# A second value copy in strips, keys interleaved on partitions, and dumps issued from SyncE in the long sequence's branch B

## The chip, the cores and the metric

The kernel runs on one core of one Trainium2 chip. The metric is the time of one execution on the device, in microseconds, as the median of several runs. The core has a matrix engine (TensorE, PE in the profile), a vector engine (VectorE, DVE), an activation engine (ScalarE, ACT), a general engine (GpSimd, POOL) and a queue engine (SyncE, SP). DMAs are issued from the queues of SP, ACT or POOL; an engine's instructions, DMA issues among them, run in the order in which they stand in its program.

## The reference

One encoder layer is computed for two sequences, a long one of 1024 tokens and a short one of 512, each with 1024 features:

```python
z = xn @ w_in                      # q_A k_A v_A q_B k_B v_B gate_A gate_B
o_a = _gqa_attention(qa, ka, va)   # 8 heads of 64, full attention
o_b = _neighbourhood_attention(qb, kb, vb, rpb)
mix = (sigmoid(ga) * (o_a @ w_proj_a) + sigmoid(gb) * (o_b @ w_proj_b)) @ w_out
h = x + mix
y = rmsnorm(h + square(relu(rmsnorm(h) @ w_up)) @ w_down)
```

Branch B is the part in question. The tokens lie on a grid 64 wide, so the long sequence has 16 rows. Each token attends, in 8 heads, to a window of 8 rows by 16 columns around it, clamped at the edges; a learned bias is added to the scores, a softmax follows, and its weights multiply the values:

```python
s = einsum('bqhd,bkhd->bhqk', qi, kb) * scale + bias
s = where(mask, s, NEG_INF)
p = softmax(s, axis=-1)
o = einsum('bhqk,bkhd->bqhd', p, vb)
```

## The kernel before

**Stages.** The two sequences are run one after the other by `run`, the short one first (`NB` = 1), the long one second (`NB` = 2); the MLP of both follows. For each sequence there are projections and sweeps of branch A for two groups of heads (`g` = 0, 1), then branch B, then the gated merge. The change touches branch B of the long sequence and, before it, its two branch A sweeps. Nearly all matrix products are made in pieces that are rounded to a high and a low part, so every operand is split first: ACT copies the high part, DVE subtracts it to get the low one.

**Values.** `values` (L637) computes the values of branch B for a tile of 128 tokens and stores them, high and low half of 64 floats each, in the DRAM tensor `vd` of tokens x 8 heads x 128. These stores go out on ACT's queue.

**Branch A's sweep** (L759 and on) works through 8 units for each group in the long sequence, 4 heads by 2 query blocks. In its gaps a `Fill` object feeds matmuls of the gates (`gate`, L439), whose weights SP loads into the three buffers of `rawp`; ACT and DVE split them.

**Branch B's units.** A unit is a head and a strip `j` of 16 query columns; its keys lie in a strip of 32 columns. The long sequence has 8 x 4 = 32 units; queries come in two halves of 128 (`hf`), each with 12 rows of 32 keys (`nkey` = 384). The loop at L1174 runs, for step `i`:

- `s_unit(i)` (L1008): POOL adds bias and mask (`bms`); TensorE makes the scores (`sbs`, four matmuls); DVE adds the bias and takes the maximum (`sbss`, `nmbs`); ACT takes Exp (`pbs`, L1065); DVE takes a reciprocal and POOL multiplies by it (L1068).
- The weights must then be turned so that keys lie on partitions. The last 8 units are turned by TensorE in `t_unit` (`ptbs`). The first 24, the set `moved`, take a **detour**: `turn` (L1072) has DVE transpose blocks of 32 x 32 (L1077) and then dumps the whole tile to DRAM (`tbs`, 384 KB, a DMA on POOL's queue, L1079); `fetch_t` (L1081) reads it back with the blocks in place (`bhs`), in four DMAs of 32 partitions on SP's queue (L1088).
- `prep_v` (L936) loads the unit's strip of values (`vss`) from `vd`, in four DMAs on SP, one for each band `a` of 32 partitions (L942). Partition `a * 32 + c` holds the key in row `4k + a`, column `c`.
- `t_unit` (L1094) splits the fetched weights, high part on ACT (L1099), low part on DVE (L1100), and `v_unit` (L1120) multiplies them with the values (`obs`).

`turn(i-1)` is called inside `s_unit(i)`, between the maxima and the Exps; `fetch_t(i-2)` comes right behind `s_unit(i)`; `t_unit` of a moved unit comes three steps after its `s_unit`, and `v_unit` one step later. Between them stand pieces of gate products (`fill.pull`) and, in two steps of every eight, the projections of the next pair of heads (`qkproj`). The buffers that matter: `pbs` has two, `bhs` three.

**What sets the order.** In branch B TensorE's order is that of the source, by hand (`mul`, L211). The orders of the other engines are made at compile time, from what each step is thought to take, and may differ from the source. `note` and `behind` (L186, L191) hold some of them: the instructions noted for an engine must come ahead of those issued inside `behind` for it. The loads of raw weights are noted for SP; the fetches and strips are issued behind them.

Of the kernel before, what the change touches and what calls it, by code (L numbers as in the profile page):

```python
# [11 lines left out]
F32 = mybir.dt.float32  # L12
# [6 lines left out]
P = 128  # L19
# [3 lines left out]
GRID_W = 64  # L23
# [38 lines left out]
def encoder(ctx: ExitStack, tc: tile.TileContext, xs, outs, w):  # L62
    nc = tc.nc
# [122 lines left out]
    def note(engine, op):  # L186
        if held_pe:
            firm[engine].append(op.ins)

    @contextmanager  # L190
    def behind(engine):  # L191
        with ExitStack() as st:
            for ins in firm[engine]:
                st.enter_context(tc.issue_after(ins))
            yield
        firm[engine].clear()
# [222 lines left out]
    def run(tr, nxt, first):  # L419
        N, x, T, NT, NB = tr.N, tr.x, tr.T, tr.NT, tr.NB  # L420
# [2 lines left out]
        halves = rows // 8  # L423

        vd = dram.tile([T, 8, P], F32, name=f"vd{N}")
        zg = [dram.tile([D, T], F32, name=f"zg{N}_{i}") for i in range(2)]
        oad = dram.tile([4 * P, T], F32, name=f"oad{N}")
        obd = dram.tile([4 * P, T], F32, name=f"obd{N}")
# [99 lines left out]
        for g in range(2):  # L528
# [230 lines left out]
            with phase(f"phA{N}_{g}") as ph:  # L759
                units = [(h, qb) for h in range(4) for qb in range(NB)]  # L760
                PP = {}

                def s_tile(u, j):
                    h, qb = u
                    nm = f"{N}_{g}_{h}_{qb}_{j}"
                    q0 = (qb * 4 + j) * P
                    lhs = qT[h % 2][:, h // 2, q0 : q0 + P]
                    s = big(f"s{nm}")[:, :T]
                    for kb in range(NB):
                        ks = slice(kb * 512, kb * 512 + 512)  # L770
                        nc.tensor.matmul(s[:, ks], lhs, kT[:, 0, ks], start=True, stop=False)
                        nc.tensor.matmul(s[:, ks], lhs, kT[:, 1, ks], start=False, stop=True)  # L772
                    nm_ = sml.tile([P, 1], F32, tag="nm", name=f"nm{nm}")
                    nc.vector.tensor_reduce(nm_, s, axis=AX.X, op=ALU.max, negate=True)  # L774
                    p = ph.tile([P, T], F32, tag="P", name=f"p{nm}", bufs=8)
                    l = sml.tile([P, 1], F32, tag="l", name=f"l{nm}")
                    nc.scalar.activation(p, s, AF.Exp, bias=nm_, accum_out=l)  # L777
                    rl = sml.tile([P, 1], F32, tag="rl", name=f"rl{nm}")
                    nc.vector.reciprocal(rl, l)  # L779
                    nc.gpsimd.tensor_scalar(p, p, rl, 1.0, op0=ALU.mult, op1=ALU.mult)  # L780
                    PP[u, j] = p

                o_of = {}

                def pv(u, kc, hi, lo):
                    h, qb = u
                    if kc == 0:
                        o_of[u] = mm(f"o{N}_{g}_{h}_{qb}")
                    o = o_of[u]
                    nc.tensor.matmul(o, vhl[:, kc, :], hi, start=(kc == 0), stop=False)  # L790
                    nc.tensor.matmul(o, vhl[:, kc, :], lo, start=False, stop=(kc == NT - 1))
                    if kc == NT - 1:
                        r0 = (g * 4 + h) * HD
                        finish_o(o, 512, oad[r0 : r0 + HD, qb * 512 : qb * 512 + 512], ph, f"A{N}_{g}_{h}_{qb}")

                for j in range(4):
                    s_tile(units[0], j)
                    fill.pull(2)
                queue = []
                LAG = 2  # L800
                for ui, u in enumerate(units):
                    h, qb = u
                    if first:
                        bias_row(g * 4 + ui)
                        if g == 0 and ui == 1:
                            early["a"] = load_a(1)
                        if g == 0 and ui == 2:
                            early["v"] = load_v(1, slot)
                    nxt_u = units[ui + 1] if ui + 1 < len(units) else None
                    sdone = 0  # L810
                    for kc in range(NT):
                        pt = mm(f"pT{N}_{g}_{h}_{qb}_{kc}")
                        for j in range(4):
                            nc.tensor.transpose(  # L814
                                pt[:, j * P : (j + 1) * P], PP[u, j][:, kc * P : (kc + 1) * P], ident
                            )
                        hi = ph.tile([P, 512], F32R, tag="pth", name=f"pth{N}_{g}_{h}_{qb}_{kc}", bufs=3)
                        lo = ph.tile([P, 512], F32R, tag="ptl", name=f"ptl{N}_{g}_{h}_{qb}_{kc}", bufs=3)
                        nc.scalar.activation(hi, pt, AF.Copy)  # L819
                        nc.vector.tensor_tensor(lo, pt, hi.bitcast(F32), op=ALU.subtract)  # L820
                        queue.append((u, kc, hi, lo))
                        if nxt_u is not None:
                            while sdone < 4 and kc >= ((0, 1, 3, 4) if NB == 2 else (0, 0, 1, 2))[sdone]:
                                s_tile(nxt_u, sdone)
                                sdone += 1

                        fill.pull(1 if NB == 1 or kc % 4 < 3 else 0)
                        if len(queue) > LAG:
                            pv(*queue.pop(0))
                fill.drain()  # L830
                for item in queue:
                    pv(*item)
# [80 lines left out]
        with phase(f"phB{N}") as ph:  # L913
# [22 lines left out]
            def prep_v(h, j):  # L936
                if h not in strips:
                    strips[h] = slot([P, 4, rows // 4, P], F32R, f"vs{N}_{h}")
                v = strips[h]
                c0 = (0, 8, 24, 32)[j]  # L940
                for a in range(4):
                    nc.sync.dma_start(  # L942
                        v[a * 32 : a * 32 + 32, j, :, :].bitcast(F32),
                        vd[:, h, :].rearrange("(k a c) d -> a c k d", a=4, c=GRID_W)[a, c0 : c0 + 32],
                    )
# [62 lines left out]
            def s_unit(u, before=None):  # L1008
# [47 lines left out]
                for hf, (sb, nm_) in enumerate(sums):  # L1056
                    nm = f"{N}_{h}_{j}_{hf}"
                    l = sml.tile([P, 1], F32, tag="l", name=f"lb{nm}")
                    p = pm[:, :, hf] if u in moved else pm[:, hf * nkey : (hf + 1) * nkey]
                    to, of = p, sb  # L1060
                    if u in moved:
                        to = p.rearrange("p b k i -> p k b i")
                        of = sb.rearrange("p (k b i) -> p k b i", b=4, i=32)
                    with behind("ACT"):
                        nc.scalar.activation(to, of, AF.Exp, bias=nm_, scale=-1.0, accum_out=l)  # L1065
                    rl = sml.tile([P, 1], F32, tag="rl", name=f"rlb{nm}")
                    nc.vector.reciprocal(rl, l)
                    nc.gpsimd.tensor_scalar(p, p, rl, 1.0, op0=ALU.mult, op1=ALU.mult)  # L1068
                    ps.append(p)
                PT[u] = pm if u in moved else ps  # L1070

            def turn(u):  # L1072

                h, j = u
                pm = PT[u]
                blocks = pm.rearrange("p b f k i -> p (b f k) i")
                tc.keep_in_program_order(nc.vector.transpose(blocks, blocks))  # L1077
                PT[u] = dram.tile([P, 4, halves * nkc * 32], F32, name=f"tb{N}_{h}_{j}")
                nc.gpsimd.dma_start(PT[u], pm.rearrange("p b f k i -> p b (f k i)"))  # L1079

            def fetch_t(u):  # L1081

                h, j = u
                hl = ph.tile([P, 2, 4, halves, nkc, 32], F32R, tag="bh", name=f"bh{N}_{h}_{j}", bufs=3)
                turned = PT[u].rearrange("(a i) b w -> b i a w", i=32)
                with behind("SP"):
                    for b in range(4):
                        nc.sync.dma_start(  # L1088
                            hl[b * 32 : b * 32 + 32, 1].rearrange("p a f k i -> p a (f k i)").bitcast(F32),
                            turned[b],  # L1090
                        )
                PT[u] = hl

            def t_unit(u):  # L1094
# [79 lines left out]
            for i in range(n + 4 - NB):  # L1174
# [8 lines left out]
                    next(pa)  # L1183
                if i < n:
                    late = i > 0 and units[i - 1] in moved
                    s_unit(units[i], partial(turn, units[i - 1]) if late else None)
                    if i > 1 and units[i - 2] in moved:
                        fetch_t(units[i - 2])
                    h, j = units[i]
                    if j == 1 and h < 7:  # L1190
                        if moved:
# [768 lines left out]
```

## Time and profile before

| what | us |
|---|---|
| median of 3 runs | 2142.17 |
| lowest, highest | 2140.59, 2144.18 |
| the profiled execution's own time | 2144.53 |
| its span, first to last instruction | 2142.7 |
| branch A of the long sequence, `g` = 0 and `g` = 1 (from the timeline) | 453 to 575, 640 to 771 |
| the 24 detour units of branch B (from the timeline) | 798 to 1000 |

The span is that of one execution taken by the hardware profiler. In its timelines a row is start, duration, engine, source line, operation, tiles written and read, count, and in brackets the idle time in front of it and what ended that. "PEld" is the loading of weights into TensorE, "SPq", "ACTq" and "POOLq" are the queues' own issues of DMAs, and "issue" stands where the profile shows nothing that was waited for. A tile's name is followed by `s`, `s1` or the like for the sequence; numbers are left out.

### The profile page before, as it was taken

To read this page: it belongs to the slowest core of one execution; us is meant where nothing else is said; L and a number is where in the kernel's file an instruction comes from. 1 tells how busy PE (TensorE), PEld (TensorE's weight loads), DVE (VectorE), ACT (ScalarE), POOL (GpSimd) and SP (SyncE) were. 2 spreads that over 40 slices of the span, in tenths; PEclk is the share of its full clock that TensorE was granted. 3 is DMA by queue.
4 is the path that set the end of the run, shared out by engine and by line. 5 is a ranking of instruction groups with operands and counts; after the bars stand their busy time and mean duration, and the time that the engine had idled before them with its cause. 6 is when DMAs were issued, how large, how long until landed. Compare 5 with 4: busy or idle time off the path is not lost.

```text
span 2142.7 us, 32014 instructions
## 1 busy us (share of the span) xinstructions
PE 2102.9 (98%) x10871; PEld 1841.3 (86%) x10871; DVE 1484.2 (69%) x2793; ACT 1141.0 (53%) x2487; POOL 374.0 (17%) x470
## 2 busy tenths in 40 slices
PE   9999999999999999989999999999999999999998
PEld 8888778988897888877888899999999988888886
DVE  6665786767657756766882877778777777659662
ACT  6664653767656645544531566566655633334442
POOL 2232310323233215533200200003000000000000
PEclk9999999999999999999999999999999999999999
DMA  6437557520122136666572666578544799688561
GB/s 190 133 97 212 156 159 252 184 73 25 54 80 70 42 95 190 206 206 184 176 247 101 209 193 192 164 252 208 159 145 158 260 353 341 213 274 279 165 206 59
DMA packets 337002, 372.95 MB, mean 174 GB/s; under 512 B 33471, under 2 KB 269639, under 8 KB 336839
## 3 DMA queue, kind: packets, MB, share of 16 engines
q1 hardware_dynamic: 296695, 296.17, 44.6%
q10 hardware_dynamic: 31072, 45.11, 6.0%
q0 software_dynamic: 9072, 29.63, 4.7%
q8 instruction: 86, 1.41, 0.3%
q14 instruction: 77, 0.63, 0.1%
HBM read 274.29 MB, written 97.32 MB: 173 GB/s over the span
## 4 chain that ended last, share of the span: by engine, by line
PE 52%; DVE 1%; issue 0%; DMA 0%; ACT 0%; SPq 0%; POOLq 0%; POOL 0%; ACTq 0%; DVEq 0%
PE dn L212 20%; PE ua L212 6%; PE ud L212 6%; PE uc L212 6%; PE ops L212 4%; PE ub L212 3%; PE ppbs L212 2%; PE ppas L212 2%; PE dnf L212 2%; PE pt L353 0%; PE obs L212 0%; PE gpss L212 0%; PE sbs L212 0%; PE ptbs L1109 0%; DVE A L1435 0%
## 5 line engine op out<-in xcount | busy, mean ns | idle before, releaser
L212 PE MATMUL dn<-wd,ah 128*128 128x512 f32 x1248 | 384.3, 389 | 0.0
L212 PEld LDWEIGHTS dn<-wd,ah 128*128 128x128 f32 x1248 | 234.3, 188 | 48.6
L212 PE MATMUL dn<-wd,al 128*128 128x512 f32 x624 | 242.8, 389 | 0.0
L1434 ACT ACTIVATE ah<-ar 128x512 fp32r<-128x512 f32 x168 | 103.9, 627 | 197.5 <-PE dn L212 186.1
L212 PE MATMUL gpss<-xs_0h,w_gs 128*128 128x512 f32 x512 | 189.7, 404 | 0.8 <-DVE ot_Bs L471 0.4
L1435 DVE TENSOR_TENSOR al<-ar,ah 128x512 fp32r<-128x512 f32 x168 | 113.8, 686 | 74.1 <-ACT ah L1434 66.9
L212 PE MATMUL ud<-B,A 128*128 128x384 f32 x768 | 143.6, 334 | 0.7 <-DVE c L1552 0.7
L212 PE MATMUL uc<-B,A 128*128 128x384 f32 x768 | 143.7, 334 | 0.0
L212 PE MATMUL ua<-B,A 128*128 128x384 f32 x768 | 138.8, 334 | 0.0
L212 PEld LDWEIGHTS dn<-wd,al 128*128 128x128 f32 x624 | 117.2, 188 | 24.2
L780 POOL TENSOR_SCALAR ps<-ps,rls 128x1024 f32<-128x1024 f32 (+1 forms) x96 | 96.9, 1010 | 225.7 <-DVE rls L779 200.4
L212 PEld LDWEIGHTS ud<-B,A 128*128 128x128 f32 x768 | 134.0, 188 | 1.1 <-DVE c L1552 1.1
L212 PEld LDWEIGHTS uc<-B,A 128*128 128x128 f32 x768 | 134.1, 188 | 0.2 <-ACT A L1434 0.2
L212 PEld LDWEIGHTS ua<-B,A 128*128 128x128 f32 x768 | 133.7, 188 | 0.2
L820 DVE TENSOR_TENSOR ptls<-pTs,pths 128x512 fp32r<-128x512 f32 x160 | 107.6, 686 | 37.7 <-ACT pths L819 36.9
L819 ACT ACTIVATE pths<-pTs 128x512 fp32r<-128x512 f32 x160 | 94.1, 598 | 73.9 <-PE pTs L814 71.6
L212 PE MATMUL ops<-wh_os,mgs 128*128 128x512 f32 x384 | 119.5, 390 | 0.0
L774 DVE TENSOR_REDUCE nms<-ss 128x1 f32<-128x1024 f32 (+1 forms) x96 | 99.8, 1040 | 25.6 <-PE ss L772 25.0
L212 PEld LDWEIGHTS gpss<-xs_0h,w_gs 128*128 128x128 f32 x512 | 97.1, 190 | 19.1 <-DVE w_gs L206 0.7
L180 POOL TENSOR_TENSOR rs_f<-ms_f,mhalf 128x1 f32<-128x1 f32 x6 | 4.0, 666 | 590.7 <-DVE ms_f L176 590.7
L777 ACT ACTIVATE ps<-ss,nms 128x1024 f32<-128x1024 f32 (+1 forms) x96 | 93.3, 972 | 22.7 <-DVE nms L774 20.1
L814 PEld LDWEIGHTS pTs<-ident,ps 128*128 128x128 f32 x640 | 77.9, 140 | 28.5 <-POOL ps L780 4.5
(288 smaller groups left out, 5158.5 us busy)
## 6 DMA issues: line engine op xcount, KB each, us to landing
ar<-ud SPq DMA_DIRECT2D x120, 512.0 KB, 5.1
br<-in_w_mlp_down_dram SPq DMA_DIRECT2D x72, 512.0 KB, 5.4
rawu<-in_w_mlp_up_dram SPq DMA_DIRECT2D x64, 512.0 KB, 4.2
ud<-c ACTq DMA_DIRECT2D x128, 192.0 KB, 2.8
raw_gs<-in_w_in_dram SPq DMA_DIRECT2D x32, 512.0 KB, 4.0
ud<-cs SPq DMA_DIRECT2D x64, 192.0 KB
tbs<-pbs POOLq DMA_DIRECT2D x24, 384.0 KB, 3.4
bhs<-tbs SPq DMA_DIRECT2D x96, 96.0 KB, 2.2
```

The costliest lines, as they stand in the source:

```text
L180: nc.gpsimd.tensor_tensor(r[:, :n], m[:, :n], mhalf[:, :n], op=ALU.pow)
L212: op = nc.tensor.matmul(out, a, b, **kw)
L774: nc.vector.tensor_reduce(nm_, s, axis=AX.X, op=ALU.max, negate=True)
L777: nc.scalar.activation(p, s, AF.Exp, bias=nm_, accum_out=l)
L780: nc.gpsimd.tensor_scalar(p, p, rl, 1.0, op0=ALU.mult, op1=ALU.mult)
L814: nc.tensor.transpose(pt[:, j * P : (j + 1) * P], PP[u, j][:, kc * P : (kc + 1) * P], ident)
L819: nc.scalar.activation(hi, pt, AF.Copy)
L820: nc.vector.tensor_tensor(lo, pt, hi.bitcast(F32), op=ALU.subtract)
L1434: nc.scalar.activation(hi, src, AF.Copy)
L1435: nc.vector.tensor_tensor(lo, src, hi.bitcast(F32), op=ALU.subtract)
```

## The change

**A second value copy.** Four DRAM tensors `vst`, one for each column strip, hold the values of the strip's 32 columns with the four row bands `a` next to each column `c`. They are filled from `vd` by DRAM-to-DRAM copies on SP, two ahead of each unit of the branch A sweeps of the long sequence: 16 for each group, 32 in all, each of 4 x 32 rows of 2 KB (256 KB).

**Keys interleaved.** Key (row `4k + a`, column `c`) now lies on partition `c * 4 + a` in place of `a * 32 + c`. So a strip is one DMA from `vst` in place of four from `vd`, and a fetch is one DMA of 128 partitions in place of four of 32, with the same bytes. For the 8 units that TensorE turns, Exp writes its result interleaved, every fourth float.

**Dumps on SP.** The dump moves from POOL's queue to SP's, behind the noted loads, and `fetch_t(i-2)` moves ahead of `s_unit(i)`; the fetch is noted, so that the dump of unit `i-1` comes behind it. The short sequence is as before.

```diff
+        vst = [dram.tile([rows // 4, 32, 4, 8, P], F32, name=f"vst{N}_{j}") for j in range(4)] if NB == 2 else None
...
                 for ui, u in enumerate(units):
                     h, qb = u
+                    if NB == 2:
+                        hs = slice(4 * g, 4 * g + 4)
+                        for a in range(2 * (ui % 2), 2 * (ui % 2) + 2):
+                            c0 = (0, 8, 24, 32)[ui // 2]
+                            nc.sync.dma_start(
+                                vst[ui // 2][:, :, a, hs, :].rearrange("k c h d -> k c (h d)"),
+                                vd[:, hs, :].rearrange("(k a c) h d -> a k c (h d)", a=4, c=GRID_W)[a, :, c0 : c0 + 32],
+                            )
...
                 v = strips[h]
+                if NB == 2:
+                    nc.sync.dma_start(
+                        v[:, j, :, :].bitcast(F32), vst[j][:, :, :, h, :].rearrange("k c a d -> (c a) k d")
+                    )
+                    return
...
-                    if u in moved:
-                        to = p.rearrange("p b k i -> p k b i")
+                    if NB == 2:
+                        if u in moved:
+                            to = p.rearrange("p b k i -> p k b i")
+                        else:
+                            to = p.rearrange("p (k i b) -> p k b i", b=4, i=32)
                         of = sb.rearrange("p (k b i) -> p k b i", b=4, i=32)
...
-                nc.gpsimd.dma_start(PT[u], pm.rearrange("p b f k i -> p b (f k i)"))
+                with behind("SP"):
+                    nc.sync.dma_start(PT[u], pm.rearrange("p b f k i -> p b (f k i)"))
...
-                turned = PT[u].rearrange("(a i) b w -> b i a w", i=32)
                 with behind("SP"):
-                    for b in range(4):
-                        nc.sync.dma_start(
-                            hl[b * 32 : b * 32 + 32, 1].rearrange("p a f k i -> p a (f k i)").bitcast(F32),
-                            turned[b],
-                        )
+                    op = nc.sync.dma_start(
+                        hl[:, 1].rearrange("p a f k i -> p a (f k i)").bitcast(F32),
+                        PT[u].rearrange("(a i) b w -> (i b) a w", i=32),
+                    )
+                note("SP", op)
...
                     late = i > 0 and units[i - 1] in moved
-                    s_unit(units[i], partial(turn, units[i - 1]) if late else None)
                     if i > 1 and units[i - 2] in moved:
                         fetch_t(units[i - 2])
+                    s_unit(units[i], partial(turn, units[i - 1]) if late else None)
```

## The prediction

> **What bounds the kernel now.** I read the page first: how busy TensorE is, and what the DMA queues move.
>
> ```profile
> span 2142.7 us, 32014 instructions
> PE 2102.9 (98%) x10871; PEld 1841.3 (86%) x10871; DVE 1484.2 (69%) x2793; ACT 1141.0 (53%) x2487; POOL 374.0 (17%) x470
> ...
> q1 hardware_dynamic: 296695, 296.17, 44.6%
> ```
>
> TensorE idles for 2142.7 - 2102.9 = 39.8 us in all; no edit here takes a matmul away, so 39.8 us plus what a lowered clock costs is all that can be won. Which part lies where the edits are? The busy time by stage says it: both sweeps of branch A in the long trunk (453 to 575 and 640 to 771 us), the 24 detour units of branch B (798 to 1000), and their tail.
>
> ```profile
> 453.00:575.00 122.00, 120.82 (x647) 98.48 (x648) 89.76 (x142) 81.29 (x145) 37.00 (x32) 1.00 0.13 39
> 640.00:771.00 131.00, 130.49 (x698) 106.17 (x697) 94.46 (x151) 86.65 (x158) 36.96 (x33) 1.00 0.18 54
> 798.00:1000.00 202.00, 192.01 (x902) 162.38 (x901) 139.39 (x335) 102.06 (x203) 89.40 (x117) 0.97 0.67 197
> 1000.00:1013.00 13.00, 10.41 (x47) 7.56 (x46) 11.39 (x25) 7.46 (x14) 5.70 (x5) 1.00 0.52 157
> ```
>
> The columns are length, then busy time of PE, PEld, DVE, ACT and POOL, granted clock, DMA share, GB/s. Branch A has 1.7 us to win and much free DMA. The detour has 10.0 us of idle time and a clock of 0.97. The waits of TensorE between 798 and 1013 us name the pieces:
>
> ```profile
> PE obs L212 <- issue: 6.8, 2, 4.7
> PE sbs L212 <- DVE kBs L1001: 2.3, 2, 1.8
> PE ppas L212 <- DVE w_pas L206: 1.5, 1, 1.5
> PE pqbs L212 <- DVE ot_Bs L471: 0.7, 1, 0.7
> ```
>
> Two waits for the weights `bhs` make up 6.8 of the 10.0 us, and the clock falls behind the longer one: 6.5 us at 0.55 cost 6.5 x 0.45 = 2.9 us.
>
> ```profile
> 943.30:949.80 6.50, 6.49 (x21) 5.69 (x22) 2.26 (x4) 1.33 (x2) 0.68 (x1) 0.55 0.76 215
> ```
>
> The timelines of PE, ACT, DVE, POOL and SP show where the 4.68 us come from (unit numbers counted along the dumps, from 0).
>
> ```profile
> 943.31 1.62 PE L212 MATMUL obs<-bhs,vss 128*128 128x256 f32 x6 [4.68 <-issue]
> ...
> 930.71 0.62 ACT L1065 ACTIVATE pbs<-sbss,nmbs 128x384 f32<-128x384 f32 x1 [0.20 <-issue]
> ...
> 940.77 0.61 ACT L1065 ACTIVATE pbs<-sbss,nmbs 128x384 f32<-128x384 f32 x1 [2.85 <-DMA tbs<-pbs]
> ...
> 941.39 0.83 ACT L1099 ACTIVATE bhs<-bhs 128x768 fp32r<-128x768 f32 x1
> ...
> 934.53 0.96 DVE L1077 STREAM_TRANSPOSE pbs<-pbs 128x768 f32<-128x768 f32 x1
> ...
> 934.30 3.15 POOL L1019 TENSOR_TENSOR bms<-rects,msks 128x384 f32<-128x384 f32 x2
> 937.40 0.57 POOL L1079 DMA_DIRECT2D tbs<-pbs  x1
> ...
> 926.34 1.73 SPq L1088 DMA_DIRECT2D bhs<-tbs  x4
> ```
>
> Read it backwards. The matmul group at 943.31 is unit 15's. Its weights were fetched by four DMAs from 926.34 on, but their rounding on ACT (L1099) stands behind the first Exp of unit 19 and runs at 941.39. That Exp waited 2.85 us until the dump of unit 17 had left its buffer (`pbs` has two). The dump was ready when the turn ended, 934.53 + 0.96 = 935.5, but it sat 1.9 us in POOL's queue behind `bms`, went out at 937.40 and landed after 3.4 us. So a **loop of two units** sets the pace: Exp 17 (930.71), scale, turn, dump, landing, Exp 19 (940.77), 10.06 us or 5.0 us a unit. TensorE, where it computes no projection, asks for one each 4.7 us:
>
> ```profile
> 861.88 0.87 PE L212 MATMUL sbs<-kBs,qBs 128*128 128x384 f32 x4
> ...
> 880.70 0.87 PE L212 MATMUL sbs<-kBs,qBs 128*128 128x384 f32 x4
> ```
>
> (four steps in 18.8 us). The spacing of `sbs` has 18 such short steps in three runs of six, with long ones of about 16 us between them, where the chain catches up.
>
> **The change, part by part.** SP's queue first: its issues in one stretch of short steps, its longest wait, the landing times of the dumps (from the tile's page), and the median landings in the detour.
>
> ```profile
> 882.49 2.27 SPq L942 DMA_DIRECT2D vss<-vds  x4
> 884.80 0.43 SPq L245 DMA_DIRECT2D raw_gs<-in_w_in_dram  x1
> ...
> 886.04 2.50 SPq L1088 DMA_DIRECT2D bhs<-tbs  x4
> ...
> SPq L1088 <- DMA tbs<-pbs: 50.2, 15, 8.2
> ...
> DMA to landing us min/median/max: 1.9/3.3/6.2
> ...
> tbs<-pbs POOLq DMA_DIRECT2D x24, 384.0 KB, 3.4
> bhs<-tbs SPq DMA_DIRECT2D x93, 96.0 KB, 2.2
> vss<-vds SPq DMA_DIRECT2D x72, 64.0 KB, 3.9
> zgs<-sgs SPq DMA_DIRECT2D x14, 256.0 KB, 3.6
> ```
>
> *One fetch and one strip a unit.* A unit costs SP 2.50 + 2.27 = 4.8 us for eight issues, as long as TensorE's step. A 512 KB load issues in 0.43 us, so size is no price; two issues cost 0.9 us and 3.9 us go. The bytes stay. It isn't on the path by itself (no PE wait names SP); I book 0 and use it as room.
>
> *Dump on SP.* POOL loses 0.57 us a unit. The dump no longer stands behind `bms` (1.9 us at unit 17), but behind the fetch two units back, now issued first, and that fetch waits for its own dump. Unit 16's dump, landing at 935.9 or earlier, lets the fetch go and then unit 17's dump by 936.4 at the latest. A dump issued from SP isn't in this trace. Bounds are 2.2 us (96 KB) and 6.2 us, the largest landing of a dump; I take 3.4, the same bytes from POOL, near the 3.6 of `zgs`. The loop becomes 10.06 - 0.57 - 1.0 = 8.5 us, 4.2 a unit, under the 4.7 asked for. So **unit 19's wait goes: -4.7 us, and -2.9 us of clock**. Next late are the two kinds of wait below it in the list; they stay. What queues behind the waiting dump: bias rectangles, strips, gate weights and stores. They had queued behind the waiting fetch already (50.2 us in 15 waits).
>
> *The first wait.*
>
> ```profile
> 933.52 0.96 PE L212 MATMUL obs<-bhs,vss 128*128 128x256 f32 x6 [2.14 <-issue]
> ...
> 931.02 0.97 DVE L1077 STREAM_TRANSPOSE pbs<-pbs 128x768 f32<-128x768 f32 x1
> 932.23 1.09 DVE L1100 TENSOR_TENSOR bhs<-bhs 128x768 fp32r<-128x768 f32 x1
> ```
>
> Unit 14's second rounding (DVE, L1100) stands behind the turn of unit 16 in DVE's order, which has no gap there; no DMA is waited for. The order is made at compile time from what each step is thought to take, so it may move; bounds -2.1 to +2.1, I book 0.
>
> *New waits.* The SP chain of dump, landing, fetch, next dump takes 3.4 + 0.45 + 0.45 = 4.3 us against 4.7: little room. I book +1.0 us, between 0 and the 1.8 of the largest small wait.
>
> *Keys interleaved for the last eight units.* Exp then writes every fourth float. The moved units' permuted Exp takes 610 ns, the last units' plain one 608:
>
> ```profile
> L1065 ACT ACTIVATE pbs<-sbss,nmbs 128x384 f32<-128x384 f32 x64 | 38.9, 610 | 41.4 <-DMA tbs<-pbs 21.2 <-DVE nmbs L1039 11.6 <-issue 3.9
> ...
> L1065 ACT ACTIVATE pbs<-sbss,nmbs 128x384 f32<-128x384 f32 x14 | 8.5, 608 | 6.4 <-DVE nmbs L1039 6.4
> ```
>
> So 0. Were it doubled, 16 x 0.6 = 10 us would land on an ACT that is 53% busy.
>
> *The second value copy.* 32 DRAM-to-DRAM copies of 256 KB on SP, 16 in each branch A sweep, where the DMA share is 0.13 to 0.18. No such copy is in the trace. Below, it costs nothing; above, see the fourth case. I take 0, as all that SP loads there is used tens of us later.
>
> **Sum**: -4.7 - 2.9 + 1.0 = -6.6 us. The profiled execution took 2144.5 us (1.8 around its span), 2.4 over the median; carried to the median, 2142.2 - 6.6 = 2135.6, said as **2135.5 us**.
>
> **Rivals.**
>
> *The order decides, not the detour (0.24).* Both waits are rows of ACT's and DVE's fixed orders: unit 15's data could be there by 931, ten us before its rounding. If the new orders put as much late elsewhere, the room on SP buys nothing: 2141 us.
>
> *SP's chain becomes the loop (0.14, slower).* A dump now waits for the landing before it. From a landing of 3.8 us on, 4.7 us a unit is broken; the dump shares SP's queue with 512 KB loads, and 6.2 us has been seen. At 4.8 us each of 18 short steps takes 5.7 instead of 4.7: +18 us, less some 3 us of lead in each of three runs: +9, so 2151 us. Against it: SP's queue is lighter by six issues a unit.
>
> *The copies hold up weights in branch A (0.12).*
>
> ```profile
> vds<-vts ACTq DMA_DIRECT2D x24, 256.0 KB, 3.2
> ...
> 647.57 0.40 SPq L245 DMA_DIRECT2D raw_bks<-in_w_in_dram  x1
> ...
> 645.85 0.33 ACTq L651 DMA_DIRECT2D vds<-vts  x1
> ...
> 699.55 1.05 ACT L199 ACTIVATE w_bks<-raw_bks 128x1024 fp32r<-128x1024 f32 x1
> ```
>
> The last value store lands at about 649; then all 16 copies of the second sweep can go. By q1's row an engine moves 296.17 MB / (0.446 x 16 x 2142.7 us) = 19.4 KB a us. If a copy, whose outermost step counts four bands of rows, runs on four engines, it takes 262 / 4 / 19.4 = 3.4 us and 16 take 54: till 703. If `raw_bks` is issued behind them it lands at 707, and ACT, in order, stands 7 us at 699.55, with 3 us of clock: +10 on the sum, 2145 us; at half that rate up to 2195. On 16 engines the copies take 14 us and nothing happens. The Trainium skill, page "DMA: Bandwidth & Descriptors", section "Why a DMA increments its semaphore by 16 and not by 1", says that a transfer is split over the largest number of engines up to 16 that divides the slowest dimension of both sides; by that it would be four here. No transfer of this trace shows it.
>
> **How the numbers follow.** Forecast 0.50. A measurement of this kernel tells some 0.2% (4.3 us) from no change. Faster: 0.50 and 0.04 of the order's case, 0.54. Same: 0.20 of that case and half of the copies', 0.26. Slower: 0.14 and the other half, 0.20. The range runs from 2129 (both `bhs` waits, the clock and the small waits gone: 6.8 + 2.9 + 3.5) to 2150, with some 0.08 below and 0.12 above.
>
> **What would show it.** Right: 24 issues each of `tbs` and `bhs` on SP, SP's short-step cost near 0.9 us, landing of `tbs` up to 3.8 us, no `obs <- issue` over 2 us, a clock of 0.98 or more in the detour. Wrong: `tbs` landing over 4 us with Exp waiting for it; ACT waiting at `w_bks` about 700 us; or idle time of 10 us in the detour under other names.

## The result, and the profile after

The changed kernel takes 2136.93 us in the median of 14 runs (2135.59 to 2138.47); the kernel before, measured beside it, 2142.49 us (2139.67 to 2144.18, 14 runs). The ratio is 0.9975, with a 95% interval of 0.9967 to 0.9983: faster by 5.6 us, just beyond what can be told from no change. The forecast of 2135.5 us was 1.4 us off. The profiled execution took 2136.87 us. The same rows of its page as those shown of the kernel before:

```profile
span 2135.0 us, 31762 instructions
PE 2099.9 (98%) x10871; PEld 1840.2 (86%) x10871; DVE 1483.2 (69%) x2793; ACT 1146.3 (54%) x2487; POOL 362.0 (17%) x446
```

Busy time by stage of the changed kernel. The columns are length, busy time of PE, PEld, DVE, ACT and POOL, granted clock, DMA share, GB/s:

```profile
575.00:640.00 65.00, 58.82 (x363) 56.76 (x362) 27.06 (x66) 31.69 (x148) 16.81 (x21) 0.95 0.33 106
...
806.00:1000.00 194.00, 190.25 (x910) 161.78 (x909) 144.07 (x351) 110.92 (x213) 84.38 (x100) 0.99 0.77 230
```

The detour's idle time fell from 10.0 us to 194.00 - 190.25 = 3.8 us and its clock rose to 0.99. But the 65 us between the two sweeps of branch A, without a gap in the kernel before, now hold 6.2 us of idle time at a clock of 0.95. This is the same stretch of the kernel before:

```profile
575.00:640.00 65.00, 65.00 (x438) 63.74 (x437) 32.30 (x79) 37.37 (x166) 18.52 (x24) 1.00 0.23 71
```

The waits of TensorE in the changed kernel's whole run (total, times, longest) name both sides:

```profile
PE zvs L212 <- ACT wh_vs L199: 5.7, 1, 5.7
PE sbs L212 <- DVE kBs L1015: 2.3, 2, 1.8
...
PE obs L212 <- DVE bhs L1117: 1.4, 2, 1.0
```

The two waits of `obs` without a named cause are gone; a wait of 5.7 us for the value weights `wh_vs` is new. Where the balance comes from is read at two milestones on TensorE's timeline, the first scores of branch B and the first output of a unit that TensorE turns itself (a group of ten matmuls). Before, then after:

```profile
798.61 0.34 PE L212 MATMUL sbs<-kBs,qBs 128*128 128x384 f32 x1
...
1017.06 1.91 PE L212 MATMUL obs<-bhs,vss 128*128 128x256 f32 x10
```

```profile
805.86 0.34 PE L212 MATMUL sbs<-kBs,qBs 128*128 128x384 f32 x1
...
1010.95 1.92 PE L212 MATMUL obs<-bhs,vss 128*128 128x256 f32 x10
```

Up to branch B the change lost 805.86 - 798.61 = 7.3 us; from there to the second milestone it won (1017.06 - 798.61) - (1010.95 - 805.86) = 13.4 us. So the total comes near the forecast as the difference of two numbers, each some 7 us away from what the sum had in its place (no cost ahead of branch B, a gain of 6.6 us in it). Both are read from one execution of each kernel, and that of the kernel before, 2144.53 us, was 2.4 us over the median in the table of before.

The loss shows on SP's queue in the changed kernel (start, duration of a run of issues, count):

```profile
452.22 134.65 SPq L808 DMA_DIRECT2D vsts<-vds  x16
586.99 4.00 SPq L245 DMA_DIRECT2D raw_vs<-in_w_in_dram  x2
...
645.51 0.63 SPq L245 DMA_DIRECT2D raw_bks<-in_w_in_dram  x1
...
655.49 136.86 SPq L808 DMA_DIRECT2D vsts<-vds  x16
```

and in the kernel before:

```profile
470.98 67.20 SPq L245 DMA_DIRECT2D raw_vs<-in_w_in_dram  x2
```

Sixteen copies kept SP for 134.65 us. The raw value weights, issued from 470.98 on before, stand behind them and go out at 586.99, after which TensorE waits 5.7 us for their rounded form. What SP waited for in the two sweeps (440 to 800 us):

```profile
SPq L808 <- DMA zgs<-sgs: 221.3, 10, 59.6
SPq L808 <- DMA oads<-os_As: 29.7, 5, 9.3
```

A copy has nothing to do with `zgs`: these are stores of gates, issued from ACT's queue through the sweep. But the DMAs of SP's and ACT's queues share eight completion counters in this program, and a copy waits until the earlier user of its counter is done; for these copies that is such a store. The longest wait, 59.6 us, ended so; the trace has this store and this copy on one counter:

```profile
527.65 0.33 ACTq L435 DMA_DIRECT2D zgs<-sgs  x1
```

```profile
529.67 0.58 SPq L808 DMA_DIRECT2D vsts<-vds  x1
```

The copy goes out 2.0 us behind the store's issue, as soon as the store has landed. SP takes its instructions in order, so it stands there until ACT has come to the store.

### The profile page after: what moved, and what is told of

The parts are those of the page before. It is cut to its first block, busy times and chain, and to the rows that moved or that the text cites. A ratio compares the mean times of both kernels' runs of the same rounds, so it can differ in the third digit from the quotient of the medians.

```text
span 2135.0 us, 31762 instructions
## 1 busy us (share of the span) xinstructions
PE 2099.9 (98%) x10871; PEld 1840.2 (86%) x10871; DVE 1483.2 (69%) x2793; ACT 1146.3 (54%) x2487; POOL 362.0 (17%) x446
## 4 chain that ended last, share of the span: by engine, by line
PE 53%; DVE 1%; issue 0%; ACT 0%; POOLq 0%; POOL 0%; ACTq 0%; DVEq 0%
PE dn L212 20%; PE ua L212 6%; PE ud L212 6%; PE uc L212 6%; PE ops L212 4%; PE ub L212 3%; PE ppbs L212 2%; PE ppas L212 2%; PE dnf L212 2%; PE pt L353 0%; PE obs L212 0%; PE gpss L212 0%; PE sbs L212 0%; PE ptbs L1126 0%; DVE A L1452 0%
```

## The experiments

Two questions follow. Theory A: the detour's gain comes from the dump on SP, as forecast, and the copies cost what SP's standing costs. Rivals: the gain belongs to the fetch as one DMA (booked at nothing), to the fetch's earlier place, or to the order made at compile time; the copies cost little. Twelve kernels, grouped by question; the ratio is to the kernel before on the same chip.

| kernel | dump on | fetch | fetch stands | copies | us | ratio, 95% |
|---|---|---|---|---|---|---|
| before | POOL | four | behind scores | none | 2142 | 1 |
| after | SP | one | ahead | narrow | 2136.93 | 0.9975 (0.9967, 0.9983) |
| `e1_late_copies` | SP | one | ahead | narrow, second sweep | 2167.44 | 1.0118 (1.0104, 1.0132) |
| `e2_wide_copies` | SP | one | ahead | wide | 2127.12 | 0.9928 (0.9915, 0.9940) |
| `e4_no_copies` | SP | one | ahead | none | 2127.55 | 0.9930 (0.9917, 0.9944) |
| `e5_copies_only` | POOL | four | behind | narrow, unread | 2172.46 | 1.0139 (1.0125, 1.0153) |
| `e7_pool_copies` | SP | one | ahead | narrow, from POOL | 2179.72 | 1.0181 (1.0167, 1.0195) |
| `e3_wide_pool_dump` | POOL | one | ahead | wide | 2133.88 | 0.9964 (0.9950, 0.9977) |
| `e6_dump_only` | SP | four | ahead | none | 2145.84 | 1.0021 (1.0012, 1.0030) |
| `e9_one_fetch` | POOL | one | ahead | none | 2129.64 | 0.9944 (0.9932, 0.9957) |
| `e10_fetch_behind` | SP | one | behind | none | 2132.93 | 0.9959 (0.9947, 0.9972) |
| `e11_one_fetch_behind_pool` | POOL | one | behind | none | 2129.88 | 0.9946 (0.9934, 0.9959) |
| `e12_four_fetch_ahead` | POOL | four | ahead | none | 2142.74 | 1.0001 (0.9992, 1.0010) |
| `e13_round_early` | POOL | four | behind | none | 2142.76 | 1.0003 (0.9994, 1.0012) |

### What the copies cost

**No copies.** The changed kernel without `vst`; a strip comes from `vd` in four DMAs, each to every fourth partition.

```diff
-                    nc.sync.dma_start(
-                        v[:, j, :, :].bitcast(F32), vst[j][:, :, :, h, :].rearrange("k c a d -> (c a) k d")
-                    )
+                    va = v.rearrange("(c a) j k d -> a c j k d", a=4)
+                    for a in range(4):
+                        nc.sync.dma_start(
+                            va[a, :, j].bitcast(F32),
+                            vd[:, h, :].rearrange("(k a c) d -> a c k d", a=4, c=GRID_W)[a, c0 : c0 + 32],
+                        )
```

> The changed kernel without the second value copy: interleaved keys, one fetch and the dump on SP as changed, but each strip again four DMAs from the first value copy, each to every fourth partition. Theory A (the copies cost 8.9 us; one DMA for a strip in place of four is only room on SP's queue): 2128 to 2131 us. Rival (the room is what takes the waits for the fetched weights away): SP issues 1.4 us more a unit, dump and fetch come late, a wait of obs over 2 us comes back, 2133 us or more.

Measured: 2127.55 us, 9.4 us under the changed kernel, as theory A has it. The strips cost nothing that the time shows, whether one DMA or four (see the next kernel, which keeps the one); the copies cost 9 us.

**Wide copies.** The same bytes, with the 32 columns outermost in place of the four row bands:

```diff
-                                vst[ui // 2][:, :, a, hs, :].rearrange("k c h d -> k c (h d)"),
-                                vd[:, hs, :].rearrange("(k a c) h d -> a k c (h d)", a=4, c=GRID_W)[a, :, c0 : c0 + 32],
+                                vst[ui // 2][:, :, a, hs, :].rearrange("k c h d -> c k (h d)"),
+                                vd[:, hs, :].rearrange("(k a c) h d -> a c k (h d)", a=4, c=GRID_W)[a, c0 : c0 + 32],
```

> The changed kernel with each copy's loop over columns (32) outside its loop over row bands (4), the same bytes in the same places. If the late value weights come from copies that run on four DMA engines (theory of the prediction's fourth case): the copies run on 16, the DMA share while they run goes from about 0.23 to over 0.5, the landing of raw_vs falls from 10.7 us to about 4, and the wait of zvs falls by 6 to 7 us: about 2129 us. If the lateness comes from SP itself, which stands in order at the copies until 587 us because they wait for stores that ACT issues later: raw_vs is issued as late as before, at most its landing is shorter; 2131 to 2137 us.

Measured: 2127.12 us. SP's queue in this kernel:

```profile
452.77 13.84 SPq L808 DMA_DIRECT2D vsts<-vds  x16
486.04 51.52 SPq L245 DMA_DIRECT2D raw_vs<-in_w_in_dram  x2
```

Sixteen copies take 13.84 us of SP in place of 134.65, and `raw_vs` goes out 101 us earlier. The time is that of the first theory, which had looked for the gain in the landing of `raw_vs` and not in its issue. Busy time in stretches of the first sweep, with narrow copies (the changed kernel; three copies on their way, then none) and with wide ones:

```profile
457.00:463.00 6.00, 5.91 (x29) 4.53 (x27) 2.98 (x7) 3.59 (x7) 3.37 (x3) 1.00 0.26 98
476.00:480.00 4.00, 4.00 (x23) 3.12 (x22) 2.93 (x4) 1.46 (x3) 0.49 (x1) 1.00 0.00 0
```

```profile
457.00:471.00 14.00, 13.90 (x69) 11.15 (x68) 9.59 (x16) 8.99 (x17) 6.80 (x6) 1.00 0.86 290
```

While narrow copies move, the DMA share is 0.26 x 16 = 4.2 engines; with wide ones it is 0.86 x 16 = 13.8, one store of 256 KB included. That agrees, closely for the four, with the section of the Trainium skill that the prediction weighed (page "DMA: Bandwidth & Descriptors", section "Why a DMA increments its semaphore by 16 and not by 1"): by its rule an outermost count of four gives four engines, one of 32 all sixteen. But the copies' speed alone doesn't make 134.65 us. At 98 GB/s sixteen copies of 262 KB would take 43 us (an estimate), and from 476 to 480 us no byte moves while SP stands at the next copy. The compiled programs of the two kernels also differ in which counters the copies wait for: the waits of copies for `zgs`, 221.3 us in ten with narrow copies, are 3.2 us in one with wide ones. No run changes the counters alone, so what the few engines would cost by themselves was not separated.

**Copies in the second sweep alone** (512 KB each, 16 in all):

```diff
-                    if NB == 2:
-                        hs = slice(4 * g, 4 * g + 4)
+                    if NB == 2 and g == 1:
+                        hs = slice(0, 8)
```

> The changed kernel with all 32 value copies' bytes moved in the second branch A sweep alone (16 copies of 8 heads, 512 KB each); none in the first. Theory A (the copies cost the changed kernel the 5.74 us wait of TensorE for the value weights of the second head group, 0.45 us behind it and 2.7 us of lowered clock, 8.9 us in all, and nothing later pays that back): 2136.9 - 8.9 = 2128 us, no wait of zvs for wh_vs over 1 us, raw_vs issued near 470 us as in the kernel before. Rival B (the wait only shows what would be lost later anyway): 2135 to 2138 us. Rival C (16 copies twice as large jam the second sweep instead): 2140 us or more, with a new wait of ACT or TensorE between 640 and 800 us.

Measured: 2167.44 us, in rival C's range. SP's timeline and TensorE's first scores in this kernel:

```profile
646.14 156.56 SPq L808 DMA_DIRECT2D vsts<-vds  x16
...
829.39 0.38 SPq L245 DMA_DIRECT2D raw_bks<-in_w_in_dram  x1
```

```profile
836.54 0.69 PE L212 MATMUL sbs<-kBs,qBs 128*128 128x384 f32 x1 [33.42 <-ACT kBs L1013]
```

SP was free only at 802.7, when branch B's loads should long have been out; the scores waited 33.42 us in one piece. It is the place of the weights in SP's queue that sets the price: `raw_bks` went out at 645.51 in the changed kernel, ahead of the second sweep's copies, and here at 829.39, behind them.

**The kernel before with the copies added, nothing reading them:**

```diff
+                            nc.sync.dma_start(
+                                vst[ui // 2][:, :, a, hs, :].rearrange("k c h d -> k c (h d)"),
+                                vd[:, hs, :].rearrange("(k a c) h d -> a k c (h d)", a=4, c=GRID_W)[a, :, c0 : c0 + 32],
+                            )
```

> The kernel before with the 32 copies added, which nothing reads. Theory A (the copies cost what they cost in the changed kernel): 2142.5 + 8.9 = 2151 us, with the same wait of zvs for wh_vs. Rival (the cost comes with the rest of the change): 2142 to 2145 us.

Measured: 2172.46 us, three times the loss expected. SP's timeline and TensorE's in this kernel:

```profile
653.02 138.85 SPq L808 DMA_DIRECT2D vsts<-vds  x16
...
799.86 0.40 SPq L245 DMA_DIRECT2D raw_bks<-in_w_in_dram  x1
```

```profile
807.73 0.80 PE L212 MATMUL pkbs<-xs_0h,w_bks 128*128 128x512 f32 x1 [20.28 <-ACT w_bks L199]
```

Here the order of SP's loads came out differently: `raw_bks` is issued behind the second sweep's copies at 799.86, and TensorE waits 20.28 us for `w_bks`. This is the mechanism of the prediction's third rival, at the load that it named. In the changed kernel the order of SP's loads has `raw_bks` ahead of those copies, and nothing is seen there.

**Copies issued from POOL:**

```diff
-                            nc.sync.dma_start(
+                            nc.gpsimd.dma_start(
```

> The changed kernel with the 32 narrow copies issued from POOL in place of SP. Theory D (the loss of the copies is SP standing in order at them, with the weight loads behind): raw_vs goes out near 470 us again and no wait of zvs over 1 us is left: 2127 to 2130 us. Rival E (the traffic on few DMA engines costs by itself, whichever queue issues it): raw_vs and other loads land late all the same, 2133 us or more.

Measured: 2179.72 us, in rival E's range, but not for its reason. SP's load of the value weights, and the longest waits of TensorE in the two sweeps (440 to 810 us):

```profile
467.27 74.83 SPq L245 DMA_DIRECT2D raw_vs<-in_w_in_dram  x2
```

```profile
PE ss L772 <- ACT ps L778: 19.2, 21, 2.7
```

With the copies off SP, `raw_vs` goes out near 470 us again and TensorE has no wait of `zvs`: this much is as theory D has it. But both sweeps are now strewn with short waits on the softmax chain, in which POOL scales `ps`. Which part is POOL's own time at the copies and which a new order was not separated, so the time of this kernel says nothing about what SP's standing costs.

### What won the time in the detour

**The dump on SP alone,** with the fetch ahead of the scores, but four fetches and keys as before:

```diff
-                nc.gpsimd.dma_start(PT[u], pm.rearrange("p b f k i -> p b (f k i)"))
+                with behind("SP"):
+                    nc.sync.dma_start(PT[u], pm.rearrange("p b f k i -> p b (f k i)"))
```

> The kernel before with the dump on SP and the fetch ahead of s_unit, all else as before: four fetches and four strips a unit, no copies. Theory A (what held the detour up is the dump's place in POOL's queue and the loop through it): 2131 to 2135 us, the wait of obs of 4.7 us gone. Rival B (SP can't carry nine issues a unit; the one fetch is what makes the move possible): about 5.2 us of issues against a step of 4.7, so waits of obs stay or grow: 2141 us or more.

Measured: 2145.84 us, no gain but 0.2% lost. The waits of TensorE between 797 and 1013 us in this kernel:

```profile
PE sbs L212 <- DVE nmbs L1039: 4.1, 1, 4.1
PE obs L212 <- issue: 2.9, 1, 2.9
PE obs L212 <- DVE bhs L1102: 2.5, 1, 2.5
```

9.5 us are back under partly new names. Theory A falls: the dump's place isn't what wins. The time is in rival B's range, but its reason, an SP that can't keep up, doesn't show at ACT, which waited little for fetched weights (797 to 1013 us):

```profile
ACT bhs L1101 <- DMA bhs<-tbs: 2.5, 2, 1.3
```

**One fetch, dump back on POOL** (the kernel without copies, with the diff above reversed):

> The run without copies (e4_no_copies, 2127.6 us), with the dump back on POOL: interleaved keys and one fetch, four strips a unit, dump on POOL. Theory A (the dump's place decides): the loop of two units stays near 10 us, a wait of obs of about 4 us and its lowered clock come back: 2138 to 2142 us. Rival B (the fetch decides: one DMA lands some 1.3 us earlier than the last of four and leaves SP free): 2127 to 2131 us.

Measured: 2129.64 us, as rival B has it, and 2.1 us over the same kernel with the dump on SP, with intervals that overlap. The gain is there without the move of the dump. With wide copies and one DMA a strip the same reversal gave:

> The run with wide copies (e2_wide_copies, 2127.1 us), with the dump back on POOL: all of the change but the dump on SP, with the copies on 16 engines. Theory A (the dump's place decides): 2138 to 2142 us. Rival B (fetch and strips decide): 2127 to 2130 us.

Measured: 2133.88 us, between the two expectations, against 2127.12, so there the dump on SP is worth 6.8 us. The two kernels of each pair ran on different chips; by the ratios to the kernel before the moves are worth 3.0 and 7.7 us. So it is between 2 and 8 us, once the fetch is one DMA, and nothing or less with four.

**The fetch's place.** Three kernels take apart the single DMA and its place in the source: the kernel without copies with the fetch behind the scores again, the kernel before with the single fetch alone, and the kernel before with the earlier place alone (`s_unit` and `fetch_t` exchanged).

> The changed kernel without the second value copy (2127.6 us), with one edit: the fetch of unit i-2 stands behind the scores of unit i again, as in the kernel before. Dump on SP, one fetch DMA, interleaved keys stay. Theory A (the single fetch DMA is what wins, where it stands in the source matters little, since the order of SP's issues is made anew): 2127 to 2131. Rival B (the fetch's earlier place wins): the fetch comes some 5 us later a unit, the loop of two units closes on it, idle time before obs returns: 2136 to 2142.

> The kernel before with one edit alone: keys interleaved so that a fetch is one DMA in place of four (strips as four DMAs, no second value copy). The dump stays on POOL, the fetch stays behind the scores. Theory A (the single fetch DMA wins by taking three issues, some 2 us a unit, out of SP's queue): 2128 to 2133, near the 2129.6 of the same kernel with the fetch moved ahead. Rival B (the fetch's place wins): 2138 to 2143, as before.

> The kernel before with one edit alone: the fetch of unit i-2, in four DMAs, stands ahead of the scores of unit i. The dump stays on POOL, keys are not interleaved. Theory A (the single fetch DMA wins): 2139 to 2145, as before. Rival B (the fetch's place wins): 2129 to 2134.

Measured: 2132.93, 2129.88 and 2142.74 us. The first lies between its two expectations, the other two are as theory A has them. **The single fetch alone wins 11.7 us** (2141.59 to 2129.88 on the same chip); the earlier place alone wins nothing, and is worth 5.4 us only with the dump on SP, where the dump stands behind the fetch (2132.93 against 2127.55). The edit of `e11_one_fetch_behind_pool` in short; interleaved Exps and strips to every fourth partition belong to it, and the fetch is noted:

```diff
-                    for b in range(4):
-                        nc.sync.dma_start(
-                            hl[b * 32 : b * 32 + 32, 1].rearrange("p a f k i -> p a (f k i)").bitcast(F32),
-                            turned[b],
-                        )
+                    op = nc.sync.dma_start(
+                        hl[:, 1].rearrange("p a f k i -> p a (f k i)").bitcast(F32),
+                        PT[u].rearrange("(a i) b w -> (i b) a w", i=32),
+                    )
+                note("SP", op)
```

In this kernel the Exps still wait for the dumps of two units earlier, and as long as before (waits of ACT from 798 to 1000 us; in the kernel before it was 21.2 us in nine waits, the longest 5.7):

```profile
ACT bhs L1110 <- DMA bhs<-tbs: 20.8, 14, 2.6
ACT pbs L1077 <- DMA tbs<-pbs: 19.8, 9, 6.8
ACT ot_Bs L470 <- PE obs L212: 11.3, 6, 5.0
```

Two further waits of ACT in the kernel before, over the same stretch:

```profile
ACT ot_Bs L470 <- PE obs L212: 27.0, 13, 4.7
...
ACT bhs L1099 <- DMA bhs<-tbs: 0.2, 1, 0.2
```

With four fetches ACT waited for fetched weights only 0.2 us, so earlier weights, or a freer SP that fetches them earlier, aren't what was missing there. What ACT waited for more than with the single fetch is TensorE's outputs: 27.0 us against 11.3. And with the single fetch TensorE never waits for `obs`. So the loop of two units through the dump is there in both, and costs only where ACT has lost its lead. Where it loses it shows at unit 17. Timelines of TensorE and ACT in the kernel before (the Exp of unit 17 is at 930.71):

```profile
922.91 0.87 PE L212 MATMUL sbs<-kBs,qBs 128*128 128x384 f32 x4
926.36 0.89 PE L212 MATMUL obs<-bhs,vss 128*128 128x256 f32 x6
```

```profile
927.28 0.59 ACT L470 ACTIVATE ot_Bs<-obs 64x512 f32<-64x512 f32 x1 [1.49 <-PE obs L212]
```

and in the kernel with the single fetch:

```profile
921.12 0.87 PE L212 MATMUL sbs<-kBs,qBs 128*128 128x384 f32 x4
924.57 0.89 PE L212 MATMUL obs<-bhs,vss 128*128 128x256 f32 x6
```

```profile
924.30 0.62 ACT L1077 ACTIVATE pbs<-sbss,nmbs 128x384 f32<-128x384 f32 x1 [0.83 <-DMA tbs<-pbs]
...
927.53 0.60 ACT L470 ACTIVATE ot_Bs<-obs 64x512 f32<-64x512 f32 x1
```

Before, ACT takes the output copy `ot_Bs` of unit 13 (computed at 926.36, at the end of unit 17's step) ahead of the Exp of unit 17, which starts 930.71 - 922.91 = 7.8 us after its scores; three roundings stand between the two as well, from 927.78 to 930.5. With the single fetch it takes them the other way round, 924.30 - 921.12 = 3.2 us after. These are ACT's fixed orders. For units 12 to 23, how many units lie between an Exp and the last output copy ahead of it, read from the compiled programs (the rows of ACT in the traces give the same):

```
unit                        12 13 14 15 16 17 18 19 20 21 22 23
before                       5  4  5  5  5  4  4  5  3  4  5  5
e12_four_fetch_ahead         5  4  5  5  5  4  4  5  3  4  5  5
e6_dump_only                 4  4  4  5  4  4  4  4  3  4  4  5
e13_round_early              4  4  4  5  5  4  4  4  3  4  4  5
e10_fetch_behind             4  4  5  5  5  5  5  5  3  4  5  5
e11_one_fetch_behind_pool    5  4  5  5  5  5  5  5  5  5  5  5
e9_one_fetch                 5  4  5  5  5  5  5  5  5  5  5  5
e2, e3, e4, after            5  5  5  5  5  5  5  5  5  5  5  5
```

A 5 asks for an output that TensorE computes right ahead of the unit's own scores. A 4 means that the Exp can't start before the end of its own unit's step on TensorE; a 3, before the end of the next step. Every kernel without copies that is not faster has 4s and a 3 from unit 17 on; those with 5s alone from there are faster by 11 us or more if they have no narrow copies, but for `e3_wide_pool_dump` (7 us). So 5s alone don't fix the time. (The three kernels with narrow copies that aren't listed: in the traces `e5_copies_only` has the row of the kernel before, `e1_late_copies` and `e7_pool_copies` have 5s throughout.) `e10_fetch_behind` stands between (9 us), and its only new wait lies after its 3:

```profile
PE sbs L212 <- DVE nmbs L1048: 3.2, 1, 3.2
```

**The rounding early, four fetches.** A last kernel forced part of that order by hand in the kernel before: the rounding of unit `k` ahead of the Exps of unit `k+3`.

```diff
-                    nc.scalar.activation(hi, lo.bitcast(F32), AF.Copy)
-                    nc.vector.tensor_tensor(lo, lo.bitcast(F32), hi.bitcast(F32), op=ALU.subtract)
+                    note("ACT", nc.scalar.activation(hi, lo.bitcast(F32), AF.Copy))
+                    note("DVE", nc.vector.tensor_tensor(lo, lo.bitcast(F32), hi.bitcast(F32), op=ALU.subtract))
...
-                due_t.setdefault(i + ls, []).append(u)
+                due_t.setdefault(i + ls - (u in moved), []).append(u)
```

> The kernel before with the order of ACT and DVE alone changed: the rounding of unit k's fetched weights stands ahead of the Exps of unit k+3, as in the kernel with one fetch DMA alone (2129.9 us), in place of k+3 or k+4 in turns. Four fetches, dump on POOL, keys as before. Theory A (the one fetch wins only because the compile-time order puts the rounding earlier; SP's issue time is no limit): 2128 to 2133, no wait of obs over 1 us. Rival B (the order isn't enough: with eight issues, 4.8 us, a unit on SP the fetched weights land too late, and ACT, which now stands at the rounding, holds up the Exps behind it): 2140 to 2155, waits of ACT for the landing of the fetch longer than the 2.6 us of the kernel with one fetch.

Measured: 2142.76 us, as before. TensorE's waits (797 to 1013 us) and ACT's timeline in this kernel:

```profile
PE sbs L212 <- DVE nmbs L1039: 5.6, 1, 5.6
PE obs L212 <- issue: 3.2, 2, 1.9
```

```profile
925.27 0.59 ACT L470 ACTIVATE ot_Bs<-obs 64x512 f32<-64x512 f32 x1 [1.49 <-PE obs L212]
...
929.56 0.62 ACT L1065 ACTIVATE pbs<-sbss,nmbs 128x384 f32<-128x384 f32 x1 [1.07 <-issue]
```

The time is that of rival B, but not its reason: ACT waited for fetched weights less than in `e11_one_fetch_behind_pool`, where it was 20.8 us in 14 waits. The page of the tile `bhs` in this kernel (idle time until, us in total, times):

```profile
  DMA bhs<-tbs: 5.3, 4
```

The forced edit moved the rounding, not the output copies, and unit 17's Exp stayed behind the output of unit 13. So moving the rounding alone isn't enough.

**What stays open.** That the single fetch wins is shown. That it wins through the place of the output copies in ACT's order is what the rows point to: which order goes with which time is shown; that the order alone would do it with four fetches isn't, since no kernel here has four fetches and a row of 5s. Nor is it separated whether the count of DMAs or the layout makes the order, since a fetch in one DMA needs the interleaved keys.

## Why the prediction was right in number and wrong in its steps

- **What bounds it**: right. The two `obs` waits and the lowered clock were what the detour could win. The wait of 4.7 us went, with its 2.9 us of clock. (The lower end of the range took the small waits as 3.5 us; the three rows listed sum to 4.5.)
- **Dump on SP, -4.7 and -2.9 us**: the wrong step. It said that the loop of two units goes under TensorE's pace because the dump leaves POOL's queue. With that alone nothing is won (2145.84 us); with the dump left on POOL 11.7 us are won, and Exp still waits up to 6.8 us for it. The loop was read rightly in the timeline, but the Exp at its start, 930.71, was taken as given. It was itself 7.8 us behind its scores, behind an output copy that stands before it in ACT's order.
- **One fetch, booked 0**: mis-sized by 11.7 us. The argument that no wait of TensorE names SP was true and beside the point: with one DMA in place of four, the compile-time order of ACT is another, and that is the likely way to the gain, though no run forced that order alone.
- **The first wait, booked 0 within 2.1 either way**: 2.1 us went with the single fetch; in the changed kernel `obs` still waits 1.4 us in two waits. **New waits, +1.0**: those 1.4 us.
- **SP's chain (rival, 0.14)**: it didn't become the loop, but not because it kept to the 4.3 us a unit of the sum. The changed kernel's trace has no landing times for its dumps; in `e4_no_copies`, with the dump on SP and one fetch too, the median landing was 4.6 us (798 to 1000 us), past the 3.8 from which the rival reckoned a loss:

```profile
tbs<-pbs SPq DMA_DIRECT2D x24, 384.0 KB, 4.6
```

  In the changed kernel SP waits for a dump's landing ahead of the fetch (806 to 1003 us), and yet TensorE waits only 1.4 us for fetched weights:

```profile
SPq L1104 <- DMA tbs<-pbs: 33.8, 17, 4.0
```

  So the lead in each run of short steps must have been larger than the 3 us that the rival gave it; no run measures it. The rival also counted SP's queue as lighter by six issues a unit; with the dump, which joins that queue, it is five.
- **Interleaved Exp, 0**: right in its cost to the time, wrong in its duration. All sixteen interleaved Exps stand in the tail; the thirteen traced from 1000 to 1100 us in the changed kernel take 987 ns in the median, not 608 (duration min/median/max):

```profile
L1082 ACT ACTIVATE pbs<-sbss,nmbs x13: 975/987/1024, 999.3 to 1047.4; 128x384 f32<-128x384 f32 x13
```

  That is 16 x 0.38 = 6 us on ACT, and no wait of TensorE names it. The moved units' permuted Exp, which the step took for a like case, writes runs of 32 floats in another order, and stays at 610 ns.
- **The copies, 0 (rival 0.12)**: cost 9 us. The rival's mechanism, weights behind the copies in SP's queue, was right, and so were its four engines. But it gave sixteen copies 54 us by their bandwidth, and they held SP for 134.65 us, by waits for ACT's stores. And it looked at the second sweep's `raw_bks`, where the first sweep's `raw_vs` was the load behind them.
- **The order decides (rival, 0.24)**: closest to the mechanism that the rows point to, but it expected an order that gives the gain back, and the new one goes with the gain.

Two mis-sized terms, -11.7 for 0 and +9 for 0, with the dump worth 2 to 8 us in place of 7.6, nearly cancelled: that the forecast came within 1.4 us was luck. The version without the copies or with wide ones (2127.55 and 2127.12 us) beats both kernels by its whole range.

## What to carry to other kernels

When a stall is followed back through an engine whose order is made at compile time, ask of the first link too why it started when it did: an edit that seems to free a queue may matter only because it remakes that order, and then one run with the edit alone is worth more than the sum. A DMA that nobody is in a hurry for still isn't free on an in-order queue: look which load stands behind it, and what the DMA itself waits for. Where a DRAM-to-DRAM copy can be written with either count outermost, try the larger: here it took 9.8 us off the changed kernel (2136.93 to 2127.12).

## What the runs showed of the hardware that was not expected

An Exp of 128 x 384 whose output goes to every fourth float took 987 ns against 608 with a plain output. Narrow DRAM-to-DRAM copies (outermost count 4) kept the DMA share at 0.26 while they moved, four of sixteen engines; with wide ones (32) of the same bytes it was 0.86. And an issue queue can be held by another engine's progress without any data between them, through completion counters that both engines' DMAs share: 221.3 us in ten waits.
